# GLU on one core: six small chained stores ahead of everything else on the scalar queue

## Chip, cores and metric

The kernel runs on one core of one Trainium2 chip. The metric is the device time of a run in microseconds. Work is divided among the core's engines: ScalarE (ACT) computes the sigmoid and issues the stores, VectorE (DVE) multiplies, SyncE (SP) issues the loads, GpSimd (POOL) does a few constants at the start, and TensorE is not used. Transfers between HBM and the on-chip memory run on 16 DMA engines. SP and ACT each have a DMA queue of their own on these engines: q1 for the loads and q10 for the stores.

## What is computed

The input is a float32 matrix of 8192 by 8192. Its left half is multiplied by the sigmoid of its right half:

```python
def reference(x):
    a, b = np.split(x, 2, axis=-1)
    return a * (1 / (1 + np.exp(-b)))
```

The output is 8192 by 4096. 268.44 MB are read and 134.22 MB written.

## The kernel before

The rows are cut into 32 tiles of 256 rows. Each of the 128 partitions holds two adjacent rows (`R = 2`), so one partition's part of a tile is a run of 64 KB of the input and of 32 KB of the output. There are two slots for input tiles (`x_sb`) and two for output tiles (`o_sb`), used in turn. `_tiles` loops over the tiles:

- L50: SP issues one load of 8 MB into the input slot. Loads 0 and 1 wait for nothing. From load 2 on, a load waits until the multiply of the tile two before it, in the same slot, is done.
- L68: ScalarE computes the sigmoid of the right halves in place. For all tiles but the first and the last this is one instruction on 128x8192 elements. The first and the last tile are cut into four pieces of 128x2048.
- L69: VectorE multiplies the left halves by the sigmoids and writes the output slot.
- L62: ScalarE's queue issues the store of 4 MB when the multiply is done. The last tile is stored in four pieces of 1 MB, each after its own multiply.

The order on each engine is that of the program. On ScalarE it is: the load of the activation table, the four sigmoids of tile 0, store 0, sigmoid of tile 1, store 1, and so on. An instruction that waits on ScalarE, a store among them, holds up all that stands behind it there. Before an output slot is written again, its last store must have landed; in odd tiles the sigmoid waits for this, in even ones the multiply.

A helper (`_launch_early`) moves load 0 ahead of the barrier with which the program starts, and another (`_close_on_sync`) makes the end of the program wait for the last store on SP.

Of the kernel before, what the change touches and what calls it, by code (L numbers as in the profile page):

```python
# [1 line left out]

# [4 lines left out]


def _tiles(ctx, tc, x, out):

    nc = tc.nc
    P = nc.NUM_PARTITIONS  # L20
    DEP = mybir.DependencyInfo(mybir.DependencyClass.Sync, mybir.DependencyReason.DATA)
    fp32 = mybir.dt.float32
    SIG = mybir.ActivationFunctionType.Sigmoid

    n_rows, n_cols = x.shape
    half = n_cols // 2
    R = 2
    SLOTS = 2
    n_tiles = n_rows // (P * R)
    x_t = x.rearrange("(n p r) m -> n p (r m)", p=P, r=R)  # L30
    out_t = out.rearrange("(n p r) m -> n p (r m)", p=P, r=R)

    pool = ctx.enter_context(tc.tile_pool(name="io", bufs=1))
    xs = [pool.tile([P, R * n_cols], fp32, name=f"x_sb{k}") for k in range(SLOTS)]
    os = [pool.tile([P, R * half], fp32, name=f"o_sb{k}") for k in range(SLOTS)]

    def implied(later, *earlier):
        for e in earlier:
            tc.declare_no_dep(later.ins, e.ins, reason="follows from the waits that are kept")

    gone = [{k: [] for k in ("loads", "sigs", "muls", "stores")} for _ in range(SLOTS)]
    last_stores = [[] for _ in range(SLOTS)]
    for i in range(n_tiles):
        old = gone[i % SLOTS]
        freed = last_stores[i % SLOTS]
        now = {k: [] for k in old}
        rows = xs[i % SLOTS].rearrange("p (r h m) -> p r h m", r=R, h=2)
        packed = os[i % SLOTS].rearrange("p (r m) -> p r m", r=R)

        load = nc.sync.dma_start(out=xs[i % SLOTS], in_=x_t[i])  # L50
        implied(load, *old["loads"], *old["sigs"])
        now["loads"].append(load)

        if 0 < i < n_tiles - 1:
            parts = [(slice(0, R), slice(0, half))]
        else:
            w = half // 2
            parts = [
                (slice(r, r + 1), slice(c * w, (c + 1) * w)) for r in range(R) for c in range(2)
            ]  # L60
        def store(cols):
            ins = nc.scalar.dma_start(out=out_t[i, :, cols], in_=os[i % SLOTS][:, cols])  # L62
            now["stores"].append(ins)

        chunks = []
        for k, (r, c) in enumerate(parts):
            b = rows[:, r, 1, c]
            sig = nc.scalar.activation(out=b, in_=b, func=SIG)  # L68
            mul = nc.vector.tensor_mul(out=packed[:, r, c], in0=rows[:, r, 0, c], in1=b)  # L69
            implied(sig, *old["sigs"], *old["muls"], *old["loads"])  # L70
            implied(mul, *old["muls"], *old["loads"], *now["loads"])
            by_sigmoid = i % 2 == 1 and len(parts) == 1
            implied(mul, *(s for s in old["stores"] if by_sigmoid or s not in freed))
            if by_sigmoid:
                for s in freed:
                    tc.add_manual_dep(sig.ins, s.ins.name, DEP, reason="frees the output slot")
            tc.keep_in_program_order(sig)
            now["sigs"].append(sig)
            now["muls"].append(mul)
            chunks.append(slice(r.start * half + c.start, r.start * half + c.stop))  # L80
            if i == n_tiles - 1 and k > 0:
                store(chunks[k - 1])
        store(chunks[-1] if i == n_tiles - 1 else slice(0, R * half))
        for s in now["stores"]:
            implied(s, *old["loads"], *old["sigs"], *old["muls"], *now["loads"], *now["sigs"])
        for k in old:
            old[k] += now[k]
        last_stores[i % SLOTS] = now["stores"]


def _launch_early(nc):

    SP = mybir.EngineType.SP
    entry, body = (b.instructions for b in nc.main_func.blocks[:2])
    load = next(i for i in body if i.engine == SP and i.opcode == "DMACopy")
    assert not load.sync_info.on_wait
    body.remove(load)
    where = next(k for k, i in enumerate(entry) if i.engine == SP and i.opcode == "Drain")  # L100
    entry.insert(where, load)


def _close_on_sync(nc):

    SP, POOL = mybir.EngineType.SP, mybir.EngineType.Pool  # L110
    ACT = mybir.EngineType.Activation
    block = nc.main_func.blocks[2].instructions
    waits = block[0]
    assert waits.engine == SP and waits.opcode == "Drain" and len(waits.sync_info.on_wait) > 1
    pool = [i for i in block if i.engine == POOL]
    drain1, gather1, release1, reset, clear, drain2, gather2, release2 = pool
    assert reset.is_reset_sema and clear.opcode == "ISA"
    others = [i for i in block[1:] if i.engine != POOL]
    arrive = [i for i in others[: len(others) // 2] if i.opcode == "Drain"]
    assert len(arrive) == 4  # L120
    body = nc.main_func.blocks[1].instructions
    last = [i for i in body if i.engine == ACT and i.opcode == "DMACopy"][-1].sync_info.on_update[0].id
    final = [w for w in waits.sync_info.on_wait if w.id == last]
    assert len(final) == 1

    def event(engine, wait, update=()):
        return mybir.InstEventSemaphore(
            name=nc.get_next_instruction_name(),
            engine=engine,
            debug=waits.debug,  # L130
            sync_info=mybir.SyncInfo(on_wait=[wait], on_update=list(update)),
        )

    n = len(block)
    for lo, hi in ((reset.reset_range_start, last), (last + 1, reset.reset_range_stop)):
        if lo < hi:
            nc.gpsimd.sem_clear(range(lo, hi))
    clears = block[n:]
    assert clears and all(i.opcode == "ISA" for i in clears)
    back = mybir.SyncUpdate(  # L140
        sync_type="semaphore",
        id=last,
        ant_name=final[0].ant_name,
        update_mode="sem-sub-imm",
        update_value=final[0].wait_value,
        update_reg=None,
    )
    block[:] = [
        *arrive,
        drain1,  # L150
        gather1,
        *(event(POOL, w) for w in waits.sync_info.on_wait if w.id != last),
        reset,
        *clears,
        drain2,
        event(SP, final[0], [back]),
    ]


@with_exitstack  # L160
def kernel(
    ctx: ExitStack,
    tc: tile.TileContext,
    x: bass.AP,
    out: bass.AP,
):
    nc = tc.nc
    with ExitStack() as pools:
        _tiles(pools, tc, x, out)
    tc.close()  # L170
    tc.compile()
    _launch_early(nc)
    _close_on_sync(nc)


# [1 line left out]
_INS = ['x']  # L177
_OUTS = [((8192, 4096), 'float32')]


# [23 lines left out]
```

## Time and profile before

| what | value |
|---|---|
| time, median of 3 runs | 933.41 us (933.29 to 933.42) |
| span of the profiled execution | 931.7 us |
| VectorE busy | 278.7 us in 38 instructions |
| ScalarE busy | 227.1 us in 39 instructions |
| one sigmoid of 128x8192 / multiply of 128x8192 | 7.03 us / 8.69 us |
| load of 8 MB, issue to landing (median) | 42.2 us |
| store of 4 MB, issue to landing (median) | 34.7 us |

The profile shows one execution, and its own time is the span; 1.7 us lie between it and the median of the runs, outside of what the span covers. Busy times are sums over the span. Times of transfers run from the issue to the landing, so they hold the time in which a transfer stands behind others on the same DMA engines.

### The profile page before, as it was taken

What the parts mean: (1) busy time and instruction counts of PE and PEld (TensorE: products, weight loads), DVE (VectorE), ACT (ScalarE), POOL (GpSimd) and SP (SyncE); (2) the same over time, 40 slices, a digit from 0 to 9 for tenths busy, and PEclk for the clock granted to TensorE, in tenths of its full rate; (3) what the DMA queues carried; (4) which work ended last, traced back from release to release, by engine and by line L of the source; (5) the groups of instructions that cost most, each with busy time, mean ns of one, the idle gap of its engine ahead of it and who ended that gap; (6) DMA issues with size and microseconds to landing.
All of it is one profiled execution on the core that took longest, in us unless ns stands there. A gap on an engine that the chain in (4) does not pass through costs nothing.

```text
span 931.7 us, 247 instructions
## 1 busy us (share of the span) xinstructions
DVE 278.7 (30%) x38; ACT 227.1 (24%) x39; POOL 0.2 (0%) x4
## 2 busy tenths in 40 slices
DVE  0333213333133331233312333123331233312333
ACT  1323330233311333113331133311333113332033
POOL 0000000000000000000000000000000000000000
DMA  9999999999999999999999999999999999999999
GB/s 405 428 450 428 422 456 405 450 428 428 450 418 438 428 436 442 428 428 450 447 408 428 442 459 428 413 460 411 450 428 425 453 408 447 428 428 450 425 430 405
DMA packets 9649, 402.67 MB, mean 432 GB/s; under 512 B 1072, under 2 KB 1072, under 8 KB 1072
## 3 DMA queue, kind: packets, MB, share of 16 engines
q1 hardware_dynamic: 4608, 268.44, 66.6%
q10 hardware_dynamic: 5040, 134.22, 33.4%
q14 instruction: 1, 0.01, 0.0%
HBM read 268.44 MB, written 134.22 MB: 432 GB/s over the span
## 4 chain that ended last, share of the span: by engine, by line
DMA 73%; DVE 15%; ACT 12%; issue 0%; ACTq 0%
DMA x_sb<-in_x_dram 73%; DVE o_sb L69 15%; ACT x_sb L68 12%; ACTq L62 0%; ACTq L68 0%
## 5 line engine op out<-in xcount | busy, mean ns | idle before, releaser
L69 DVE TENSOR_TENSOR o_sb<-x_sb 128x8192 f32<-128x8192 f32 (+1 forms) x38 | 278.7, 7344 | 647.1 <-ACT x_sb L68 647.1
L68 ACT ACTIVATE x_sb<-x_sb 128x8192 f32<-128x8192 f32 (+1 forms) x38 | 225.8, 5952 | 695.6 <-DMA x_sb<-in_x_dram 694.4
L68 ACT ACT_TABLE_LOAD x1 | 1.3, 1283 | 0.8 <-PEq L188 0.8
L188 POOL MEMSET const-bfloat16-1.0<- 128x1 bf16 x1 | 0.1, 102 | 0.0
L188 POOL MEMSET const-uint8-127<- 128x1 uint8 x1 | 0.1, 102 | 0.0
L188 POOL MEMSET const-float32-0.0<- 128x1 f32 x1 | 0.1, 99 | 0.2 <-issue 0.2
L188 POOL MEMSET const-float32-1.0<- 128x1 f32 x1 | 0.1, 99 | 0.0
## 6 DMA issues: line engine op xcount, KB each, us to landing
out_dram<-o_sb ACTq DMA_DIRECT2D x31, 4096.0 KB, 34.7
out_dram<-o_sb ACTq DMA_DIRECT2D x4, 1024.0 KB, 5.6
x_sb<-in_x_dram SPq DMA_DIRECT2D x32, 42.2
```

The source lines that it names most:

```text
L68: sig = nc.scalar.activation(out=b, in_=b, func=SIG)
L69: mul = nc.vector.tensor_mul(out=packed[:, r, c], in0=rows[:, r, 0, c], in1=b)
L188: nc = _bacc.Bacc("TRN2", target_bir_lowering=False, num_devices=1)
```

## The change

At the start of `_tiles`, before the loop, a tile of zeros (16 partitions of 128 float32, 512 bytes each) is set by VectorE. ScalarE's queue then issues six stores of it, each to the first 128 columns of output rows 0 to 15. All six write the same bytes of the output, so each waits for the one before it to have landed. Store 0 writes the same rows later, with their right values, and waits for the sixth. The six stores are kept ahead of ScalarE's other instructions in program order, the table load included.

```diff
@@ -37,6 +37,12 @@
     def implied(later, *earlier):
         for e in earlier:
             tc.declare_no_dep(later.ins, e.ins, reason="follows from the waits that are kept")
+
+    zeros = pool.tile([16, P], fp32, name="zeros")
+    nc.vector.memset(zeros, 0.0)
+    for _ in range(6):
+        warm = nc.scalar.dma_start(out=out[0:16, 0:P], in_=zeros)
+        tc.keep_in_program_order(warm)
 
     gone = [{k: [] for k in ("loads", "sigs", "muls", "stores")} for _ in range(SLOTS)]
     last_stores = [[] for _ in range(SLOTS)]
```

In the changed kernel the small stores are line L44, the memset L42, the loads L56, the stores L68, the sigmoids L74 and the multiplies L75. The rest is as it was.

## The prediction

> **What bounds the kernel now.** I read the page first: busy rows, then DMA.
>
> ```profile
> span 931.7 us, 247 instructions
> DVE 278.7 (30%) x38; ACT 227.1 (24%) x39; POOL 0.2 (0%) x4
> DMA  9999999999999999999999999999999999999999
> ...
> HBM read 268.44 MB, written 134.22 MB: 432 GB/s over the span
> ```
>
> No engine is busy for a third of the span, and the DMA row is full in every slice. The bytes set the time: 402.7 MB at 432 GB/s. A wait costs nothing as long as the 16 DMA engines have packets queued, and costs its full length once they have none. The windows show where they were less than full (start and length, busy time of DVE, ACT and POOL, clock, DMA share, GB/s):
>
> ```profile
> 0.00:21.95 21.95, 0.00 (x0) 1.28 (x1) 0.20 (x4) 1.00 1.02 430
> 21.95:44.80 22.85, 8.90 (x4) 7.32 (x5) 0.00 (x0) 1.00 0.94 390
> 44.80:102.80 58.00, 17.39 (x2) 14.06 (x2) 0.00 (x0) 1.00 1.00 434
> 102.80:872.60 769.80, 234.64 (x27) 189.84 (x27) 0.00 (x0) 1.00 1.00 435
> ```
>
> From 44.8 on it is the same 434 to 435 GB/s. So the change, which sits in the first microseconds, must be judged in the first two rows. The timeline of that stretch:
>
> ```profile
> 0.78 1.28 ACT L68 ACT_TABLE_LOAD   x1 [0.78 <-PEq L188]
> 21.95 7.31 ACT L68 ACTIVATE x_sb<-x_sb 128x2048 f32<-128x2048 f32 x4 [19.89 <-DMA x_sb<-in_x_dram]
> 23.89 8.90 DVE L69 TENSOR_TENSOR o_sb<-x_sb 128x2048 f32<-128x2048 f32 x4 [23.89 <-ACT x_sb L68]
> 32.82 0.38 ACTq L62 DMA_DIRECT2D out_dram<-o_sb  x1
> 44.80 7.03 ACT L68 ACTIVATE x_sb<-x_sb 128x8192 f32<-128x8192 f32 x1 [15.53 <-DMA x_sb<-in_x_dram]
> ```
>
> Loads 0 and 1 are issued at 0.00 and 0.78. ScalarE idles 19.89 us until load 0 lands. Tile 0 takes 32.82 - 21.95 = 10.87 us of compute, and only then do store 0 and load 2 go out (two x slots). The waits confirm it:
>
> ```profile
> ACT x_sb L68 <- DMA x_sb<-in_x_dram: 694.4, 32, 22.3
> SPq L50 <- DVE o_sb L69: 859.9, 30, 31.7
> ```
>
> Last, the packet records of the trace. A load is 8 packets of 64 KB on each engine, 2.42 us each. Load 0's first packets start 1.00 us after its issue and take up to 3.3 us, 0.8 over the rest. Its last packets end at 21.0 to 21.6 and the semaphore packet (9 ns) lands 0.35 us later. Without any other transfer load 1 would follow with 8 x 2.42 = 19.3 us, so **the engines run dry at 40.9 unless load 2 or store 0 is there**. With 1.0 us from issue to first packet, tile 0 must be done by 39.9: 7.1 us of slack over 32.82.
>
> Store 0 is the one store that meets an empty scalar queue under load traffic. Issued at 32.82, its first packet starts at 38.81, 6.0 us later. The load packet in flight (33.1 to 35.5) ends, another load packet runs first, and that one takes 3.3 us instead of 2.42: a stall of 0.87 us on all engines, seen at no other store. From there loads and stores alternate packet by packet, the semaphore packets taking turns of their own.
>
> **What the Trainium skill says.** "DMA: Bandwidth & Descriptors", section "Queues, rings and completion order": each DMA engine goes round-robin between queue rows, a packet at a time. The trace agrees: 64 KB of load (2.42 us), 32 KB of store (1.21 us), in turn. The same page, "Anatomy of one DMA", puts about 2.0 us of fixed cost on a DMA of GpSimd's path, mostly the write receipt. The trace's hardware queue shows 1.0 us ahead of the first packet and 0.33 to 0.35 us from semaphore packet to landing, for stores too; I use these. "ScalarE: Activation LUTs", "What ACT_TABLE_LOAD costs": about 1283 ns; the trace has 1.28 us.
>
> **The change part by part.** Nothing is removed. (1) A 16x128 memset on VectorE. No such row; the nearest are POOL's 128x1 memsets at 0.10 us. VectorE idles until 23.89, so it costs nothing but 0.1 to 0.3 us ahead of the first small store. (2) Six stores of 16 rows of 512 bytes on ScalarE's queue, ahead of the table load. In the built program the first waits for the memset, and each later one for the DMA semaphore of the one before: five full round trips in which ScalarE can do nothing else. Six issues at 0.35 us each (L62's 0.34 to 0.38), one packet per DMA engine and store, some 0.03 us (8 KB takes 0.31 us). Bytes: 48 KB, 0.1 us. (3) Behind the waiting stores stand the table load (1.28 us, until now hidden in the 19.89 us of idling) and sigmoid 0; behind it VectorE's multiplies, and behind those store 0 and load 2. (4) Store 0 also waits for the sixth small store, long landed by then, and DMA semaphores shift their numbers; load 2's new semaphore wait is on small store 1. Both cost nothing.
>
> The price of a round trip is not in the profile; store 0's start is the nearest. **Both ends:** with no stall and the queue switched at the next packet edge, a link is the rest of the running load packet, the small packet, one load packet before the semaphore's turn: 2.42 + 0.03 + 2.42 = 4.9 us (the 0.35 of landing, the wake-up and the 1.0 of start lie inside the first 2.42). As store 0 met it, one more load packet and 0.87: 8.15 us. A link whose start takes longer than 1.0 us misses an edge: 10.6 us. I take 8.15, because that is what this queue showed with this traffic.
>
> The sum then: store 1 is issued at 0.95 and arrives at about 1.95. The second load packet ends at 7.08 on the last engine, + 0.87 stall, + 2.42, + 0.35: it lands at 10.75. The others follow at 8.15, but one link is 2.4 us shorter, since the semaphore packet of load 0 takes a turn: 18.9, 24.65, 32.8, 40.95. Store 6 is out at 41.35, the table loaded at 42.65, and **sigmoid 0 starts at 42.65 instead of 21.95**, 20.7 later. Tile 0 ends at 53.5; load 2 and store 0 are issued there. Their first packets start at 54.5, slower by 0.8 as load 0's were: full flow from 55.3. Before, the same work had full flow at 40.9 + 0.87 = 41.75. **Shift 13.55 us.** It consists of 5 stalls (4.35) with the engines empty from 45.3 to 54.5 (9.2), 0.8 of restart, less the 0.87 that store 0 no longer meets.
>
> Does it come back later? Load 1 has landed by then, so tile 1 follows tile 0 directly, and load 3 is issued 15.8 us (7.04 + 8.70) after load 2, which needs 29 us in its share. In the steady state the next load also comes about 13 us before the one in flight ends (60.58 against 73.6). The queues are never empty again, and no slack is left to win time back. At the end the last store is issued at 925.8 with 5.5 us of packets still queued; the tail also moves as a whole.
>
> The span is one profiled execution, 931.7; the median of the runs is 933.41, 1.7 more. 931.7 + 13.6 = 945.3, so **947.0 us** as a median, 1.5% slower. What this kernel's measurement can tell from no change is taken as 0.2%, 1.9 us.
>
> **The rivals.** *Hidden under load 0 (not slower).* If links are 4.9 us (the first 6.5, from 0.95 to 7.45), the fifth lands at 26.9, sigmoid 0 starts at 28.6 and tile 0 ends at 39.5, inside the 39.9. The turning point is the fifth landing at 27.3, a mean of 5.3 us for the five links. For it: 0.87 may be a cold start of the queue, paid once, and store 0's 6.0 us may come from load 2 being issued in the same instant (32.818 and 32.822). Against it: no record shows a small DMA under load that fast. 933.4 to 934.5. *Stall without the extra packet:* links of 5.75 us, tile 0 ends near 42 to 44, just as load 1, itself delayed by the stalls, runs dry at about 46. Left are the stalls, 6 x 0.87 less one: 938. *Extra packet without stall:* links 7.3, sigmoid 0 at 38.3, tile 0 at 49.2, full flow at 51.0: + 9.3 to 10, 943. *Missed edge:* links of 10.6 until load 1 ends, then fast: tile 0 ends near 60, + 20, 953 to 957. *Faster* would need DMA idle time to remove; before there is only the start and the 0.87, under 0.2%. That the stores aren't chained is excluded by the waits in the program.
>
> **How the numbers follow.** As summed 0.46 (945 to 950); hidden 0.12; stall alone 0.18; extra packet alone 0.12; missed edge 0.10; faster 0.02. Range 936.5 to 954: it holds the first, third and fourth and the lower part of the fifth, and leaves out the hidden case. Faster 0.02, same 0.12, slower 0.86.
>
> **What would show it.** In the profile after: L44's issue-to-landing median (8 us as summed; 5 in the hidden case); start of the first sigmoid (42.7; under 29.3 hidden); GB/s of the page's third slice (46.6 to 69.9) near 290 (7.9 of its 23.3 us empty); issue of load 2 near 53.5; 435 GB/s from then on, and the same 17 us from last load to end give or take 3. If sigmoid 0 starts late but the time stays, the slack argument is wrong; if the DMA shows no gap before load 2 yet the time grows, the stalls are it.

## The result and the profile after

The changed kernel takes **943.95 us** (median of 4 runs, 943.79 to 944.15) against 933.41 us: a ratio of 1.0111, 95% interval 1.0098 to 1.0124. It is 10.5 us slower. The forecast was 947.0 with a range of 936.5 to 954.

The page of the kernel after, its span, busy times, DMA row, GB/s and bytes:

```profile
span 942.5 us, 258 instructions
DVE 278.8 (30%) x39; ACT 227.0 (24%) x39; POOL 0.2 (0%) x4
DMA  9699999999999999999999999999999999999999
GB/s 415 299 378 421 446 421 446 421 446 421 446 419 449 417 451 413 455 410 458 410 458 407 458 406 462 406 462 406 462 406 462 406 462 406 456 410 458 410 455 389
...
HBM read 268.44 MB, written 134.27 MB: 427 GB/s over the span
```

No engine works longer than before. The single new thing in the DMA row is the 6 in the second slice, with 299 GB/s. The windows, cut where the packet records say that the DMA engines stop and start, show what it is (start and length, busy time of DVE, ACT and POOL, clock, DMA share, GB/s):

```profile
0.00:21.95 21.95, 0.17 (x1) 0.00 (x0) 0.20 (x4) 1.00 1.03 431
21.95:41.00 19.05, 0.87 (x1) 4.10 (x3) 0.00 (x0) 1.00 0.89 387
41.00:50.00 9.00, 8.02 (x4) 5.02 (x4) 0.00 (x0) 1.00 0.00 0
50.00:102.80 52.80, 17.38 (x2) 13.53 (x2) 0.00 (x0) 1.00 1.03 436
102.80:872.60 769.80, 226.32 (x27) 189.79 (x27) 0.00 (x0) 1.00 1.00 433
...
923.10:942.50 19.40, 8.99 (x4) 7.47 (x4) 0.00 (x0) 1.00 0.95 405
```

For 9 us nothing at all is moved, while ScalarE and VectorE compute tile 0. Before and after that the rate is nearly the old one. The chain of waits tells why tile 0 is late (start, length, what was waited for or done; "issue" is time in which the engine waited for nothing that the profile shows):

```profile
1.06 8.77 DMA out_dram<-zeros
9.83 0.02 issue
9.85 7.21 DMA out_dram<-zeros
17.06 0.02 issue
17.08 5.05 DMA out_dram<-zeros
22.14 0.02 issue
22.16 7.09 DMA out_dram<-zeros
29.25 0.02 issue
29.27 7.25 DMA out_dram<-zeros
...
36.89 1.28 ACT L74
...
38.19 1.92 ACT x_sb L74
...
40.13 8.91 DVE o_sb L75 x4
...
49.06 0.37 ACTq L68
```

These are the five round trips: 8.77, three near 7.2, and one of 5.05. Then comes the table load, and sigmoid 0 at 38.19 instead of 21.95. Store 0 and load 2 go out at 49.06 instead of 32.82, both 16.24 later.

The packet records of the 16 DMA engines close the account. Between their packets they idle 9.8 us more than before, all of it in this one gap. Packets that take longer than usual cost 1.07 us more per engine, from two sources. Load 2's first packets take 3.5 to 3.9 us on most engines instead of 2.42, on average 1.10 too long; before, the packets ahead of store 0 were 0.87 too long, so this is 0.23 more. And from 60 us on, 349 of the stores' 32 KB packets take up to 0.1 us longer than their 1.21, which none did before: 0.86 per engine. The small packets add 6 x (27 + 9) ns = 0.22. In all that is 11.1; the last packets end 10.97 later, on average over the engines (930.97 and 941.94), the span is 10.8 longer, and the median of the runs 10.5.

Past the gap the tiles also keep time in another way. A store of 4 MB now takes 42.3 us to land (median) instead of 34.7, and in 14 tiles, the odd ones from 3 to 29, what ScalarE waits for last is the store that frees the output slot, where before it was the load in every tile (total us, times, longest):

```profile
ACT x_sb L74 <- DMA x_sb<-in_x_dram: 352.6, 16, 25.0
ACT x_sb L74 <- DMA out_dram<-o_sb: 310.1, 14, 22.2
```

In sum these waits are no longer than the 694.4 us for loads before, and the DMA engines have packets queued all the while: the rate of this stretch is 433 GB/s against 435.

### The profile page after: what moved, and what is told of

Same layout as the page of the kernel before. It is cut to its first block, busy times and chain, and to the rows that moved or that the text cites. A ratio compares the mean times of both kernels' runs of the same rounds, so it can differ in the third digit from the quotient of the medians.

```text
span 942.5 us, 258 instructions
## 1 busy us (share of the span) xinstructions
DVE 278.8 (30%) x39; ACT 227.0 (24%) x39; POOL 0.2 (0%) x4
## 4 chain that ended last, share of the span: by engine, by line
DMA 71%; DVE 16%; ACT 12%; issue 0%; ACTq 0%
DMA out_dram<-o_sb 63%; DVE o_sb L75 16%; ACT x_sb L74 12%; DMA x_sb<-in_x_dram 4%; DMA out_dram<-zeros 4%; ACT L74 0%; ACTq L68 0%; ACTq L44 0%; DVE zeros L42 0%
## 5 line engine op out<-in xcount | busy, mean ns | idle before, releaser
L75 DVE TENSOR_TENSOR o_sb<-x_sb 128x8192 f32<-128x8192 f32 (+1 forms) x38 | 278.6, 7344 | 654.5 <-ACT x_sb L74 654.5
L74 ACT ACTIVATE x_sb<-x_sb 128x8192 f32<-128x8192 f32 (+1 forms) x38 | 225.7, 5950 | 667.9 <-DMA x_sb<-in_x_dram 352.6
L42 DVE MEMSET zeros<- 16x128 f32 x1 | 0.2, 165 | 0.9 <-PEq L194 0.9
## 6 DMA issues: line engine op xcount, KB each, us to landing
out_dram<-o_sb ACTq DMA_DIRECT2D x31, 4096.0 KB, 42.3
```

What stands on the lines that cost most here:

```text
L42: nc.vector.memset(zeros, 0.0)
```

## The experiments

Two theories were set against each other. **Round trips:** ScalarE is held, and time is lost only while the DMA engines have nothing to do. **Traffic:** the small stores cost DMA time themselves. A third question was what a round trip consists of. Times of before in the same comparisons had medians of 933.28 to 933.68.

**Fewer stores.**

```diff
-    for _ in range(6):
+    for _ in range(3):        # and 4, and 5
```

Three: 

> Three small chained stores instead of six. Round-trip theory (ScalarE is held by the waits for the landings; what is lost is only the time in which the DMA engines stand empty because load 2 and store 0 come late): the third is issued at 17.1, the table is loaded by 18.7, before load 0 lands at 21.95, so sigmoid 0 starts at 21.95 and the time is that of before, 933.3 to 933.8. Traffic theory (the small stores cost time on the DMA engines themselves, whoever waits): half of the 10.5 us, 938 to 939. Beside it: store 0 then meets a queue that has already been used. If the 0.87 us stall on the load packet ahead of it was the queue's first use, that packet now takes 2.4 us; if not, about 3.3 us again.

Four: 

> Four small chained stores. Round-trip theory with the slack of the prediction: the fourth is issued at 22.1, sigmoid 0 starts late, at 23.8 instead of 21.95, tile 0 is done at 34.7, but the DMA engines have load 1 until 41, so load 2 still comes in time and the 1.8 us of delay cost nothing: 933.3 to 934.0. If any delay of ScalarE costs its length, 935.3. Traffic theory: four sixths of 10.5, 940.5.

Five: 

> Five small chained stores instead of six. Round-trip theory: the fifth is issued at 29.3, sigmoid 0 starts at 30.9, tile 0 is done at 41.8, load 2's first packets come at 42.8 to 43.9, and the DMA engines stand empty for about 2.5 us instead of 9.8; one link of 7.27 us less is 7.3 us less time: 936.7 (936 to 937.5). Traffic theory: five sixths of 10.5, 942.2.

| small stores | last of them issued at | sigmoid 0 | load 2 issued | time, us | ratio (95%) |
|---|---|---|---|---|---|
| 3 | 17.0 | 21.92 | 32.8 | 933.70 | 1.0003 (0.9994 to 1.0011) |
| 4 | 22.3 | 23.92 | 34.8 | 933.87 | 1.0004 (0.9995 to 1.0013) |
| 5 | 29.2 | 30.85 | 41.7 | 936.87 | 1.0040 (1.0025 to 1.0055) |
| 6 | 36.5 | 38.19 | 49.1 | 943.95 | 1.0111 (1.0098 to 1.0124) |

Not a slope by the number of stores, but a threshold. With four, sigmoid 0 is late and nothing is lost, which the windows of that kernel show: no stretch without transfers. In its packet records no DMA engine idles for as long as 0.3 us in this time.

```profile
0.00:23.30 23.30, 0.17 (x1) 0.67 (x1) 0.20 (x4) 1.00 0.97 406
23.30:46.60 23.30, 8.90 (x4) 9.34 (x6) 0.00 (x0) 1.00 1.03 426
46.60:69.90 23.30, 8.69 (x1) 5.61 (x1) 0.00 (x0) 1.00 0.97 421
```

From five to six nearly each microsecond of delay is one of time: load 2 is 7.3 later, the time 7.1 longer. The traffic theory is out. But with five the loss, 3.4 us, isn't idle time alone. In the packet records of that kernel the DMA engines idle 2.3 us, load 2's first packets take 3.9 to 4.6 us on 15 of the 16, and 269 store packets are longer, as in the changed kernel.

The run with three also settles that the 0.87 us stall isn't the first use of the queue: three stores had used it, and the load packets ahead of store 0 again took 3.2 to 3.5 us.

**The same stores without the chain.**

```diff
-    for _ in range(6):
-        warm = nc.scalar.dma_start(out=out[0:16, 0:P], in_=zeros)
+    for j in range(6):
+        warm = nc.scalar.dma_start(out=out[0:16, j * P : (j + 1) * P], in_=zeros)
```

> Six small stores of the same size to six different pieces of the same 16 rows, so that none waits for another; all else as in the changed kernel. Round-trip theory: ScalarE only pays six issues, done by about 3.5, sigmoid 0 starts at 21.95, and the time is 933.3 to 934.0. Traffic theory: the same packets, so about 943 to 944.

933.72 us, ratio 1.0002 (0.9994 to 1.0011). The timeline shows six issues in 2.73 us and a table load that is done long before load 0 lands:

```profile
1.05 2.73 ACTq L44 DMA_DIRECT2D out_dram<-zeros  x6
3.82 1.28 ACT L74 ACT_TABLE_LOAD   x1 [3.82 <-issue]
22.09 7.31 ACT L74 ACTIVATE x_sb<-x_sb 128x2048 f32<-128x2048 f32 x4 [16.99 <-DMA x_sb<-in_x_dram]
```

Same bytes, same packets, no loss that the runs can tell (0.25 us): the cost of the change is its waits. The stores still take 8.8 to 28.4 us to land, only nobody waits for them.

**Longer chain.**

```diff
-    for _ in range(6):
+    for _ in range(8):
```

> Eight small chained stores; the seventh and eighth go out when load 1 is through. Theory that a link is long only because of the load packets ahead of it: the seventh is issued at 41.6, the eighth 1.4 us later at 43.0, sigmoid 0 starts at 44.7, tile 0 is done at 55.5, 6.5 us later than with six: 950.4 (949.5 to 951.5). Theory of a constant price per link (about 7 us): two more links, 956 to 958.5.

950.53 us, ratio 1.0182 (1.0165 to 1.0199), where 950.4 was expected. One more thing differs here: load 1 is issued at 9.86 instead of 0.78, because it waits for the first small store; load 0 keeps the DMA engines busy until 21.6, so this opens no gap. The chain of waits has the seventh link, after load 1 is through, at a fifth of the others:

```profile
36.55 5.02 DMA out_dram<-zeros
41.56 0.02 issue
41.58 1.34 DMA out_dram<-zeros
```

**The chain on idle DMA engines.**

```diff
         implied(load, *old["loads"], *old["sigs"])
+        if i < 2:
+            tc.add_manual_dep(load.ins, warm.ins.name, DEP, reason="the loads after the small stores")
...
-    _launch_early(nc)
```

> Loads 0 and 1 wait until the sixth small store has landed, so that the chain runs on idle DMA engines; load 0 is no longer ahead of the starting barrier. Packet-turn theory: no load packets to wait for, a link of 1.4 to 1.6 us (1.0 from issue to packet, 0.35 to landing), the loads go out at about 10, and everything is later by that: 943 to 944. Fixed-latency theory: links of about 7 us here too, the loads out at 44: 976 to 978.

942.63 us, ratio 1.0098 (1.0083 to 1.0113). The groups of instructions on the tile of zeros give the landings, here first and then in the changed kernel:

```profile
DMA to landing us min/median/max: 1.3/1.4/1.4
```

```profile
DMA to landing us min/median/max: 5.0/7.2/8.8
```

A small store alone takes 1.4 us; the other 5.8 of its 7.2 us in the changed kernel come from the loads beside it. The loads go out at 9.4, and the time is 9.4 longer than that of before beside it (933.28). Six round trips ahead of everything (9.4) cost about as much as the same chain beside the loads (10.5).

**Smaller load packets.** Loads 0 and 1 go to a padded slot, so that each partition's 64 KB come as four packets of 16 KB:

```diff
-    xs = [pool.tile([P, R * n_cols], fp32, name=f"x_sb{k}") for k in range(SLOTS)]
+    xs = [pool.tile([P, R * n_cols + 32], fp32, name=f"x_sb{k}") for k in range(SLOTS)]
...
+        if i < 2:
+            x_sb = xs[i % SLOTS].rearrange("p (c m) -> p c m", c=2 * R)[:, :, :half]
+            src = src.rearrange("p (c m) -> p c m", c=2 * R)
...
```

> The changed kernel, with loads 0 and 1 written to a padded input slot so that their packets are 16 KB (about 0.6 us) instead of 64 KB; later loads as they were. Packet-turn theory (a small store waits for the load packet in flight, one more, and one before its semaphore packet): a link of 3.2 to 3.6 us instead of 7.27, the sixth store issued at 18 to 20, sigmoid 0 at about 22. Fixed-latency theory (it takes some 3 us or more from the issue until a DMA engine sees the small packet, however the loads are cut): links of 4.3 to 5 us, the sixth issued at 23 to 26. Time by either: sigmoid 0 starts early enough, 933.3 to 935.

The same cutting without small stores: 

> The kernel before with the same padded slot and 16 KB packets in loads 0 and 1, without any small stores: what the cutting does alone. Both theories: no change, 933.2 to 934.2, sigmoid 0 at 21.9 to 22.2.

Neither theory had the size. In the packet records the semaphore packet follows the small one after 0.63 us, as one 16 KB packet between them explains (2.44 with 64 KB). But from the issue to the small packet it still takes 3.3 to 3.8 us on the first engine and 4.1 to 5.2 on the last, as with 64 KB (3.6 to 3.8 and 4.3 to 4.5, after the first store). On idle engines it is 0.8 to 1.0. So what a new store stands behind is not a number of packets: in either case at least 2.5 us pass on top, about as long as 64 KB of load take on one DMA engine (2.42), which is one packet of the long kind or four of the short. The landings:

```profile
DMA to landing us min/median/max: 5.2/5.6/6.1
```

The sixth was issued at 30.4, tile 0 was done at 42.9 and the time was 936.94 (ratio 1.0039, 1.0025 to 1.0053), not the 933.3 to 935 that both theories had. Without small stores the cutting gave a median of 934.61 (19 of the 20 runs between 933.87 and 936.07, one at 968.54; ratio of the 19 1.0014, 1.0007 to 1.0021), against an expected 933.2 to 934.2, and sigmoid 0 at 22.56 instead of 21.9 to 22.2. So some 1.3 of the 3.7 us that the kernel with small stores lost come with the cutting alone. The packet records without small stores show two parts of this: the first packets start 0.4 us later, and 310 of the stores' packets are longer, by 0.8 us per engine.

**The chain on GpSimd's queue.**

```diff
-        warm = nc.scalar.dma_start(out=out[0:16, 0:P], in_=zeros)
+        warm = nc.gpsimd.dma_start(out=out[0:16, 0:P], in_=zeros)
```

> The six chained stores on GpSimd's queue instead of ScalarE's, so that the chain is as long but ScalarE isn't held ahead of sigmoid 0. Round-trip theory: sigmoid 0 starts at 21.95, load 2 is issued at 32.8, store 0 waits for the sixth landing at about 41 to 46, load 2 keeps the DMA engines busy in the meantime: 933.3 to 935. Traffic theory, or a cost of the chain as such: 943 to 944.

The mechanism was as expected, the time was not. The timeline has sigmoid 0 on time, load 2 is issued at 32.7, and store 0 goes out at 48.08, after the sixth landing:

```profile
21.88 7.31 ACT L74 ACTIVATE x_sb<-x_sb 128x2048 f32<-128x2048 f32 x4 [19.81 <-DMA x_sb<-in_x_dram]
...
39.04 0.48 POOL L44 DMA_DIRECT2D out_dram<-zeros  x1 [7.04 <-DMA out_dram<-zeros]
48.08 0.37 ACTq L68 DMA_DIRECT2D out_dram<-o_sb  x1
```

The DMA engines have no gap around 41 to 50. But 12 of the 20 runs lie between 933.29 and 945.56 with a median of 937.5 (ratio of these 1.0042, 1.0023 to 1.0060), and the other eight, over 1.5% above the fastest, reach 970.05. In the profiled run, of 939.51, 15 DMA engines end within 0.3 us of 932.5 and one at 937.7. Between 60 and 900 us, 72 of its load packets are longer than usual, by 9.2 us in all, where the trace of before has one, by 0.24. The records don't name the DMA engine of a packet, so it isn't shown that these packets fell on the late one. That a run with the full chain can take 933.29 agrees with the round-trip theory; what lengthens the others isn't settled, and a cost of the chain on this queue isn't excluded by this experiment.

**The stall.** Two kernels looked at the load packet ahead of a small store of another shape: three stores of 8 KB per row, and one store of 128 rows of 512 bytes.

```diff
-    zeros = pool.tile([16, P], fp32, name="zeros")
+    zeros = pool.tile([16, 16 * P], fp32, name="zeros")   # and [P, P], one store
...
```

> Three chained small stores, but of 8 KB per row instead of 512 bytes (one packet of 0.31 us per DMA engine). Looked at is the load packet ahead of each small store. If the 0.87 us stall ahead of store 0 goes with the length of the packet that a store reads, those packets take 2.6 us or more instead of 2.42; if it goes with the number of packets in the store, or with something else of store 0, they take 2.42. Time as before either way, about 933.5 to 935.

> A single small store of 128 rows of 512 bytes, so eight packets and a semaphore packet on each DMA engine, as store 0 has, but 27 ns long instead of 1213. Looked at is the load packet ahead of the first of them (the second or third of load 0). If the 0.87 us stall goes with the number of packets that a store brings, that load packet takes about 3.3 us; if it goes with their length, 2.42. Time as before within 0.3 us plus at most the stall, 933.4 to 934.8.

With eight packets of 512 bytes per engine the load packet ahead takes 2.42 us, so it isn't the number of packets. With 8 KB packets eight of sixteen load packets ahead of the second store took 2.47 to 2.64, those ahead of the other two 2.42, so neither branch of the expectation holds. Ahead of store 0, with 32 KB packets, all sixteen take 3.1 us and more in both kernels. That fits a stall that grows with the length of the packets that the store reads, but doesn't show it: sizes between were not tried, and store 0 differs in more than this, as in its 4 MB. The times were 934.80 and 933.51, one run each.

## Why the prediction was right, and where a term was off

**What bounds the kernel: right.** The DMA engines set the time, and the change had to be judged in the first 50 us. The rate from 102.8 to 872.6 is 433 GB/s against 435.

**The mechanism: right.** ScalarE held by five round trips, table load and sigmoid 0 behind them, load 2 late, DMA engines empty, nothing won back. The kernels with three, four and five stores show the slack: the prediction had tile 0 due by 39.9; done at 34.8 it was free, at 41.7 it cost 3.4 us, more than the 1.8 that it was over, for the longer packets that the experiment with five shows. That one link is 2.4 us shorter, because load 0's semaphore packet takes a turn, is the 5.05 in the chain: there the semaphore packet of the small store follows its data after 0.03 us, with the end of load 0 at 20.9 to 21.6, and not after 2.44.

**The step that was off is the price of a link.** I took store 0's start for that of a small store, stall included: 8.15 us. Measured: 7.2, which is the sum without the stall, 2.42 + 2.42 + 0.03 + 2.42 = 7.29. In the changed kernel no load packet ahead of a small store was longer than 2.42. That was the rival "extra packet without stall", at 943 and with a chance of 0.12; the measured 943.95 lies closest to it, and the case that the median was built on, with a chance of 0.46, did not happen. In terms of the sum:

| term | predicted | measured |
|---|---|---|
| fifth landing | 40.95 | 36.52 |
| sigmoid 0 | 42.65 | 38.19 |
| load 2 issued | 53.5 | 49.05 |
| stalls ahead of small stores | 4.35 | 0, and 0.22 of small packets |
| DMA engines empty | 9.2 | 9.8 |
| restart, less the stall before | 0.8 - 0.87 | 1.10 - 0.87 |
| longer store packets from 60 us on | not in the sum | 0.86 |
| sum | 13.55 (the rounded parts give 13.48) | 11.1 (10.5 in the runs) |

The empty time came out nearly right for two reasons that cancel: the chain was 4.4 us shorter, but without stalls load 1 was also through 4.3 us sooner (41.0, not 45.3). So the stalls were 4.1 too many, and against that stand 0.6 of empty time, 0.3 of restart and 0.9 of longer store packets that the sum lacked. That these took back nearly half of the error is luck. The restart was taken from load 0's first packets (0.8 over); load 2's, with store 0 beside them, were 1.1 to 1.5 over on most engines.

The signs shifted with the link: L44's median was 7.2 for 8, sigmoid 0 came at 38.2 for 42.7, load 2 at 49.05 for 53.5. So the empty stretch lies across the page's second and third slices (299 and 378 GB/s), not in the third alone, for which some 290 had been named.

**The cover of the other parts: right.** The memset took 0.165 us on an idle VectorE. The tail from the last load's landing took 19.4 us (17.0 before), within the 17 give or take 3. The range held because it reached over the bounds of the link, 4.9 to 10.6.

## What to carry to other kernels

A small transfer that someone waits for costs a round trip past other packets on the same DMA engines: 1.4 us here when they were idle, 7.2 beside loads of 64 KB packets. Price a chain of waits by its links under that load, and then ask what the delayed engine would have issued and by when the DMA engines need it: up to that moment the delay is free (four links, 933.87), past it it counts in full or somewhat more (five, 936.87; six, 943.95). The same stores without the waits cost nothing that could be measured (933.72).

## What was not expected of the hardware

- Cutting the loads from 64 to 16 KB packets did not bring a new store's first packet forward: 3.3 us at the least after its issue, against 0.8 on idle engines. In either case at least 2.5 us more pass. Whether this is an amount of load data ahead of it or a delay under load isn't told apart, since at a steady rate both are the same.
- Small stores of 512 bytes met no stall on load packets; store 0, with packets of 32 KB, did in every kernel in which it met running loads on an otherwise empty store queue. Beside 64 KB load packets it was 0.7 to 1.2 us in one packet on each of the 16 engines; with four small stores it was spread over two packets, 0.8 to 1.7 in sum. It was there also where load 2 had been issued 15 us earlier (the chain on GpSimd's queue, 3.1 to 3.4 us per packet). So the stall is neither the queue's first use nor load 2's issue in the same instant.
- With the chain on GpSimd's queue even the 12 runs within 1.5% of the fastest spread over 12 us, where those of before spread over 1.3 at most.
- The longer store packets from 60 us on came with ScalarE's waits for the output slot in the changed kernel, in that with five stores and in both with cut loads (349, 269, 357 and 310 packets). But with eight stores, and with the chain on GpSimd's queue, the same waits are there and only 18 and 15 store packets are longer. What brings them is open.
